# The MLP of a hybrid decoder layer on one core: order of the early products, engine of the weight sums, steps of splits and loads

## The chip, the cores and the metric

One core of a Trainium2 chip. The metric is device microseconds of one execution of the whole layer, the median of several runs. The engines are TensorE (PE: matmuls, and its weight loads PEld), VectorE (DVE, `V` in the code), ScalarE (ACT, `S`), GpSimd (POOL, `G`) and SyncE (SP, `SY`), which issues all the DMAs of this kernel. Each engine takes its instructions in the order in which the program gives them, so an instruction that waits holds up all that stand behind it on its engine.

## The reference

One decoder layer on 1024 tokens of width 1024, in float32: an attention mixture and an RWKV-7 branch, merged by gates, then a squared-ReLU MLP of width 4096, then a gated embedding per layer. The change touches the MLP alone:

```python
h = h + rmsnorm(merged @ w_out[i], mix_post_norm[i])
f = rmsnorm(h, ffn_pre_norm[i])
f = jnp.square(jax.nn.relu(f @ w_ff_in[i])) @ w_ff_out[i]   # 1024x1024 @ 1024x4096, 1024x4096 @ 4096x1024
h = h + rmsnorm(f, ffn_post_norm[i])
e = (p[i] @ w_ple[i]) * jax.nn.sigmoid(h @ w_ple_gate[i])
h = h + rmsnorm(e, ple_post_norm[i])
```

## The kernel before

**Precision.** Each float32 operand is split into a high part, rounded by ScalarE (`S.activation(hi, raw, Copy)` into fp32r), and a low part, `raw - hi`, by VectorE or GpSimd. A product is three matmuls (`mm3`, L289: high by high, high by low, low by high; lines 292, 294, 296), each 128x128 by 128x512.

**Seven products.** Both layers of the MLP are cut in two by two blocks and multiplied with seven products in place of eight, over sums of blocks. The hidden width is cut into 16 rows p of 256 (`NP`). In the first layer the products of a row are 1 and 2, and then 6, 5, 7, 3, 4 (`SEQ`), of four times three matmuls each. Products 1 and 2 need only tokens 0 to 511 and unchanged weights, so they are made early for all rows (`early`, L1555), while tokens 512 to 1023 are still on their way through `mixed` and `put_f`. 27 of the 32 come before anything else of the MLP, and the last five between the products of row 0. The outcome of product 1 goes to memory (`p1_scr`), product 2 is added to it in the same PSUM bank, and the result, after relu and square, goes to `c_scr`. So a bank is held from (p,1) to (p,2). Before, the order is (p,1), (p+1,1), (p,2), (p+1,2), and three banks take turns (`bank`, L1244).

`put_f` (L1418) makes, for each tile of 128 tokens from 512 on, the operands F[3] to F[7] out of the transposed tile: sums on VectorE (d, t2) and GpSimd (c, t4, two steps each), and a split of each by ScalarE and one of the two.

**The main loop** (`mlp`, L1652) goes over p = 1 to 15. TensorE makes row p's five other products in 20 chunks of three matmuls (`chunks`, L1631; `first`, L1598), and between them the second layer of row e = p - 1. For even e that is seven products over four token tiles (`seven`, L1828), for odd e four plain ones in eight steps u of two tiles (`plain`, L1847). Results go to five PSUM banks in turn (`XB`, L1825), from which VectorE adds them to totals in SBUF (tile `tot`). The first product of `FIRST` takes a new bank for each of the four token tiles.

`prep(n + 2)` (L1798), at the start of product n, prepares operands two products ahead into one of three pairs of tiles (`rooms`): the left one from `operand` (L1778; sums of blocks of hidden values on VectorE), split by ScalarE and GpSimd; the right one, for products 6, 5, 7 and 4, loaded from `bs_scr`, where `w2_sums` (L1755) had put the split sums of blocks of w_ff2's rows. `w2_sums` runs in six parts for the next even row during the plain products: parts 0 and 3 make two sums each on GpSimd, the others split one sum and store it. For p = 0 it runs in `beside` (L1576), among the early products.

**Deferred work.** What must not hold up an engine at once goes on the list `pend`; `flush` (L1481) runs the list after every chunk and every token tile. `part` (L1868) fills pauses with work for the end of the layer: it loads a piece of other weights (x = 0) and one step later splits and stores it (x = 1; ScalarE, VectorE, SP), through the two buffers of tile tag "gst". `take` (L1646) loads the next row's hidden values so far, `load_w2` (L1733) a row's two tiles of w_ff2, `w1_raw` and `w1_sum` the blocks of w_ff_in and their sums, `last_split` (L1717) the operands of the last row, whose second layer is `ff2_last` (L1888).

**Order.** A planner (`Order`, L136) emits all this with estimated times: dense work, and chains beside it that start when due (`yield` of a time). It sets TensorE's order throughout, and SP's from the early products on; with row 0's first product (L1663) all engines follow the written order.

Of the kernel before, what the change touches and what calls it, by code (L numbers as in the profile page):

```python
# [244 lines left out]
def layer(ctx: ExitStack, tc: tile.TileContext, x, pT, wz, wup, w_out, wff1, w_ff2, w_ple, w_pleg,  # L245
# [1151 lines left out]
    def mixed(i, ps):  # L1397
# [83 lines left out]
    def flush():  # L1481
        while pend:
            pend.pop(0)()
# [26 lines left out]
    for p in range(0, NP, 2):  # L1510
        early_ += [(p, 1), (p + 1, 1), (p, 2), (p + 1, 2)]
# [14 lines left out]
    def w1_split(j):  # L1526
# [7 lines left out]
        lo = lambda: (V if j < NA and j % 4 == 3 else G).tensor_tensor(w[:, 1], src, w[:, 0], OP.subtract)  # L1534
# [20 lines left out]
    def early(j):  # L1555
# [8 lines left out]
        if i == 1:  # L1564
            A_[p] = bank()
# [8 lines left out]
        SY.dma_start((p1_scr if i == 1 else c_scr)[p], dst)  # L1574

    def beside(j):  # L1576
# [10 lines left out]
        if j == 19:  # L1587
            load_w2(0)
# [4 lines left out]
        if j in (24, 26, 27, 28, 30, 32):  # L1593
            w2_sums(0, (24, 26, 27, 28, 30, 32).index(j))
# [57 lines left out]
    def mlp():  # L1652
# [11 lines left out]
        last["turn"].__enter__()  # L1664
        for n in range(5):
# [8 lines left out]
        flush()  # L1674
        for p in range(1, NP):
            Y["n"] = 0
            e = p - 1
            if e % 2 == 0:
                for x in range(7):
                    yield from chunks((20 * x + 23) // 7 if p < NP - 1 else (3, 6, 9, 13, 17, 20, 20)[x])  # L1680
                    yield from seven(items.index((e, x)))
                    if x == 0:
                        load_w2(p)
                    if x == 4:
                        take(p + 1)
                    if p == NP - 1:
# [6 lines left out]
            for u in range(8):  # L1693
                yield from chunks((20 * u + 23) // 8)
# [9 lines left out]
        flush()  # L1704
# [12 lines left out]
    def last_split(k, hs, ws):  # L1717

        if k not in last:
            if k == 0:  # L1720
                last["h"] = rtile([128, 4, 512], "lh", "BK", F32R)
                last["w"] = [rtile([128, 1024], "lw", t, F32R) for t in ("r", "k")]
            last[k] = (rtile([128, 2, 512], "lhl", ("Ep", "En")[k], F32R),
                       rtile([128, 1024], "lwl", ("kk", "MP")[k], F32R))
        for h in hs:
            x = 2 * k + h
            S.activation(last["h"][:, x], raw_h[NP - 1][:, x], AF.Copy)
            V.tensor_tensor(last[k][0][:, h], raw_h[NP - 1][:, x], last["h"][:, x], OP.subtract)
        for _ in ws:
            SY.dma_start(last["w"][k].bitcast(F32), pk[2][:, k, 0])  # L1730
            SY.dma_start(last[k][1].bitcast(F32), pk[2][:, k, 1])

    def load_w2(p):  # L1733
        if p == NP - 1:
            return
        raw_w[p] = [rtile([128, 1024], "w2r", ("r", "k", "MP")[(2 * p + k) % 3]) for k in range(2)]
# [18 lines left out]
    def w2_sums(p, n):  # L1755
# [6 lines left out]
        if n == 0:  # L1762
            G.tensor_tensor(t1, b[1], b[0], OP.subtract)
            G.tensor_tensor(t2, b[3], t1, OP.subtract)
            return
        if n == 3:
            G.tensor_tensor(t1, b[3], b[1], OP.subtract)
            G.tensor_tensor(t2, b[2], t2, OP.subtract)
            return
        x = n - 1 - (n > 3)  # L1770
        d = split2((t2, t1, t1, t2)[x], rooms(p)[1][x % 2], G)
        if p == 0:
            flush()
# [397 lines left out]
```

## Time and profile before

| | |
|---|---|
| timed runs | 1838.38, 1847.18, 1848.96 us; median 1847.18 |
| profiled execution | 1837.83 us, span 1836.0 us |
| PE | 1753.1 us busy (95%) |
| DVE, ACT, POOL | 1051.2 (57%), 751.6 (41%), 776.8 (42%) us busy |
| granted clock of TensorE, mean | 0.983 |
| DMA queue of SP | 240.98 MB, 38.0% of 16 engines' time |

A view of the profile lists the instructions by line of the code and tile names, `out<-in`; all of ACT, DVE and POOL's have line L113, the planner's helper, so they are told apart by their tiles: `wa`, `wr`, `w2r` are raw weights of the first and second layer, `wh`, `wl` split first-layer weights, `f`, `c`, `d`, `t` the tiles of `put_f`, `pa` the copies of early products, `duo` a split operand of the second layer, `sum` a sum of blocks, `bs` the store of split sums, `hr` hidden values, `gp`, `gph` the pieces of `part`. A wait is written "waiter <- who ended it". A stretch without stalls shows what TensorE needs for a matmul, and a window's length less its count times that is what it lost.

### The profile page before, as it was taken

To read this page: it belongs to the slowest core of one execution; us is meant where nothing else is said; L and a number is where in the kernel's file an instruction comes from. 1 tells how busy PE (TensorE), PEld (TensorE's weight loads), DVE (VectorE), ACT (ScalarE), POOL (GpSimd) and SP (SyncE) were. 2 spreads that over 40 slices of the span, in tenths; PEclk is the share of its full clock that TensorE was granted. 3 is DMA by queue.
4 is the path that set the end of the run, shared out by engine and by line. 5 is a ranking of instruction groups with operands and counts; after the bars stand their busy time and mean duration, and the time that the engine had idled before them with its cause. 6 is when DMAs were issued, how large, how long until landed. Compare 5 with 4: busy or idle time off the path is not lost.

```text
span 1836.0 us, 26373 instructions
## 1 busy us (share of the span) xinstructions
PE 1753.1 (95%) x10084; PEld 1417.0 (77%) x10084; DVE 1051.2 (57%) x1799; ACT 751.6 (41%) x1377; POOL 776.8 (42%) x532
## 2 busy tenths in 40 slices
PE   9999999999999999999998799998999989898998
PEld 8887777878877777778787687877877768676887
DVE  6289768586443333436538404575666756657743
ACT  5824423513244434534424544333343333333453
POOL 1343221221222323332303767767677676773211
PEclk9999999999999999999999999999999999999999
DMA  4521122113332222335413474546455464456611
GB/s 157 204 92 36 50 78 89 45 59 109 112 110 72 58 58 81 113 131 175 146 49 101 162 264 165 188 140 241 165 178 178 154 234 157 163 181 258 240 40 53
DMA packets 99392, 242.66 MB, mean 132 GB/s; under 512 B 11329, under 2 KB 11713, under 8 KB 98754
## 3 DMA queue, kind: packets, MB, share of 16 engines
q1 hardware_dynamic: 99266, 240.98, 38.0%
q8 instruction: 79, 1.29, 0.3%
q14 instruction: 47, 0.39, 0.1%
HBM read 167.14 MB, written 67.11 MB: 128 GB/s over the span
## 4 chain that ended last, share of the span: by engine, by line
PE 63%; DVE 10%; DMA 8%; POOL 8%; ACT 5%; issue 4%; SPq 1%; POOLq 0%; DVEq 0%; ACTq 0%
PE z L294 13%; PE z L296 13%; PE z L292 13%; PE bk L292 4%; PE bk L294 4%; PE bk L296 4%; DMA duo<-bs 2%; DVE tot L113 2%; DMA hr<-cscr 2%; POOL duo L113 2%; SPq L132 1%; POOL wh L113 1%; POOL wl L113 1%; PE sc L275 1%; DVE g L113 1%
## 5 line engine op out<-in xcount | busy, mean ns | idle before, releaser
L292 PE MATMUL z<-uh,wh 128*128 128x512 f32 (+1 forms) x800 | 313.0, 391 | 6.2 <-ACT part L113 3.0
L294 PE MATMUL z<-ul,wh 128*128 128x512 f32 (+1 forms) x800 | 314.7, 393 | 1.3 <-DVE ul L113 1.3
L296 PE MATMUL z<-uh,wl 128*128 128x512 f32 (+1 forms) x800 | 313.2, 392 | 2.7 <-POOL wl L113 2.7
L113 POOL TENSOR_TENSOR wl<-wr,wh 128x1024 fp32r<-128x1024 f32 (+1 forms) x56 | 133.0, 2375 | 420.9 <-ACT wh L113 401.7
L113 DVE TENSOR_TENSOR tot<-tot,bk 128x512 f32<-128x512 f32 x336 | 217.5, 680 | 52.6 <-PE bk L296 52.4
L292 PEld LDWEIGHTS z<-uh,wh 128*128 128x128 f32 x800 | 151.6, 189 | 37.4 <-ACT part L113 3.5
L296 PEld LDWEIGHTS z<-uh,wl 128*128 128x128 f32 x800 | 151.6, 190 | 34.3 <-POOL wl L113 4.0
L294 PEld LDWEIGHTS z<-ul,wh 128*128 128x128 f32 x800 | 151.7, 190 | 32.1 <-issue 3.6
L292 PE MATMUL bk<-duo 128*128 128x512 f32 x224 | 94.9, 424 | 33.1 <-DMA duo<-bs 16.9
L113 ACT ACTIVATE wh<-wr 128x1024 fp32r<-128x1024 f32 (+2 forms) x94 | 81.0, 861 | 100.9 <-PE z L294 55.9
L113 ACT ACTIVATE hr<-hr 128x512 f32<-128x512 f32 x96 | 60.7, 632 | 134.0 <-DVE hr L113 132.5
L113 POOL TENSOR_TENSOR duo<-sum,duo 128x512 fp32r<-128x512 f32 x64 | 89.0, 1395 | 25.6 <-ACT duo L113 24.9
L113 DVE TENSOR_TENSOR gp<-gp,gph 128x512 fp32r<-128x512 f32 x28 | 32.9, 1175 | 115.8 <-ACT gph L113 92.3
L113 ACT ACTIVATE duo<-sum 128x512 fp32r<-128x512 f32 x64 | 39.9, 623 | 135.3 <-POOL sum L113 77.0
L294 PE MATMUL bk<-duo 128*128 128x512 f32 x224 | 91.8, 410 | 1.6 <-POOL duo L113 1.6
L296 PE MATMUL bk<-duo 128*128 128x512 f32 x224 | 91.6, 409 | 0.0
L292 PE MATMUL bk<-ws,duo 128*128 128x512 f32 x224 | 87.1, 389 | 0.0
L294 PE MATMUL bk<-ws,duo 128*128 128x512 f32 x224 | 87.1, 389 | 0.0
L296 PE MATMUL bk<-ws,duo 128*128 128x512 f32 x224 | 87.1, 389 | 0.0
L292 PEld LDWEIGHTS bk<-duo 128*128 128x128 f32 x224 | 44.2, 197 | 55.6 <-DVE tot L113 25.0
L113 DVE TENSOR_TENSOR hr<-hr,z 128x512 f32<-128x512 f32 x80 | 54.3, 679 | 51.0 <-PE z L296 29.2
L292 PE MATMUL z<-f,wh 128*128 128x512 f32 x212 | 83.1, 392 | 0.0
(364 smaller groups left out, 4212.8 us busy)
## 6 DMA issues: line engine op xcount, KB each, us to landing
wr<-in_wz_dram SPq DMA_DIRECT2D x48, 512.0 KB, 3.7
bs<-duo SPq DMA_DIRECT2D x32, 512.0 KB, 3.0
duo<-bs SPq DMA_DIRECT2D x32, 512.0 KB, 4.1
w2r<-in_w_ff_dram SPq DMA_DIRECT2D x30, 512.0 KB, 6.4
wr<-in_wff_dram SPq DMA_DIRECT2D x56, 256.0 KB, 4.4
hr<-p1scr SPq DMA_DIRECT2D x48, 256.0 KB, 6.7
xt<-in_x_dram SPq DMA_DIRECT2D x16, 512.0 KB, 3.8
gscr<-gst SPq DMA_DIRECT2D x32, 256.0 KB, 2.1
```

The lines of the kernel that those rows point to most:

```text
L113: return f(*a, **kw)
L132: self.eng.dma_start(out_, in_)
L275: PE.matmul(out_, a, b, start=start, stop=stop)
L292: PE.matmul(ps, ah, bh, start=start and i == 0, stop=False, skip_group_check=not start)
L294: PE.matmul(ps, ah, bl, start=False, stop=False, skip_group_check=not start)
L296: PE.matmul(ps, al, bh, start=False, stop=i == n - 1, skip_group_check=not start)
```

## The change

The diff, cut:

```diff
@@ mixed, put_f
+        yield from wait(lambda: i < 5 or i - 1 in t_f)
         yield from put_f(hh, i)
...
         for n, x, eng in ((7, d, V), (6, t2, V), (5, c, G), (4, t4, G)):
+            if n in (6, 5):
+                yield 2.0
             S.activation(at(n, 0), x, AF.Copy)
@@ flush
-        while pend:
-            pend.pop(0)()
+        run = pend[:]
+        pend.clear()
+        for job in run:
+            job()
@@ early products
-    for p in range(0, NP, 2):
-        early_ += [(p, 1), (p + 1, 1), (p, 2), (p + 1, 2)]
+    for p in range(0, NP, 4):
+        early_ += [(p + q, i) for i in (1, 2) for q in range(4)]
...
-        lo = lambda: (V if j < NA and j % 4 == 3 else G).tensor_tensor(w[:, 1], src, w[:, 0], OP.subtract)
+        eng = V if k is not None and (j > 20 or j % 4 == 3) else G
+        lo = lambda: eng.tensor_tensor(w[:, 1], src, w[:, 0], OP.subtract)
...
-            A_[p] = bank()
+            if p == 0:
+                za, zb, zc = (("z0", "z1", "s0")[(zn[0] + n) % 3] for n in (1, 2, 3))
+                A_["tags"] = ("s1", "s2", "s3", za, zb, "s1", "s2", "s3", zc, za, zb, "s1", "s2", "s3", "s1", zc)
+            A_[p] = psum.tile([128, 512], F32, name="bk", tag=A_["tags"][p])
@@ sums ahead
+    AHEAD = (4, 2, 0)
+    steps = [(0, -1), (0, 0), (1, -1)] + [(0, n) for n in range(1, 6)] + [(1, 0), (2, -1)] + [
+        (1, n) for n in range(1, 6)] + [(2, n) for n in range(6)]
+    def ahead_(n):
+        for _ in range(n):
+            if steps:
+                q, x = steps.pop(0)
+                if x < 0:
+                    load_w2(AHEAD[q], ("kk", "v") if q == 1 else ("r", "k"))
+                else:
+                    w2_sums(AHEAD[q], x, ("a", "px", "Ep", "En"))
+                    for _ in range(3):
+                        flush()
@@ beside
-        if j == 19:
-            load_w2(0)
...
-        if j in (24, 26, 27, 28, 30, 32):
-            w2_sums(0, (24, 26, 27, 28, 30, 32).index(j))
+        if sch.t > t_f.get(7, 1e9) + 2.0:
+            ahead_(2 if j % 3 == 0 else 1)
+        if j == NA + 9:
+            ahead_(99)
@@ mlp, even e (seven products)
-                    if x == 0:
+                    if x == 2:
                         load_w2(p)
...
                     if p == NP - 1:
+                        if x in (0, 1):
+                            last_w(x, 0, "rk"[x])
                         if x in (1, 2, 5):
                             e_weights((1, 2, 5).index(x))
+                        if x == 4:
+                            last_w(0, 1, "En")
+                            last_w(1, 1, "MP")
+                            last_split(0, (0, 1))
                         if x == 5:
-                            last_split(0, (0, 1), (0,))
-                            last_split(1, (1, 0), (1,))
+                            last_split(1, (1, 0))
@@ mlp, odd e (four plain products)
             for u in range(8):
+                if u % 2 == 0:
+                    flush()
+                    part(2 * p - 4 + u // 2, 0)
                 yield from chunks((20 * u + 23) // 8)
-                if u == 0:
+                if u == (2 if p in AHEAD else 0):
                     load_w2(p)
                 yield from plain(items.index((e, u // 2)), u % 2)
-                if u == 1:
+                if u == 3:
                     take(p + 1)
-                    w2_sums(p, 0)
-                if 0 < u < 6:
-                    w2_sums(p, u)
-                part(2 * p - 4 + u // 2, u % 2)
+                if p in AHEAD:
+                    if u == 3:
+                        fetch(p, 6)
+                else:
+                    if u == 1:
+                        w2_sums(p, 0)
+                    if 0 < u < 6:
+                        w2_sums(p, u)
+                if u % 2:
+                    part(2 * p - 4 + u // 2, 1)
@@ w2_sums (all four sums and the low halves: G becomes V; the store is put off by two flushes)
-            G.tensor_tensor(t1, b[1], b[0], OP.subtract)
-            G.tensor_tensor(t2, b[3], t1, OP.subtract)
+            V.tensor_tensor(t1, b[1], b[0], OP.subtract)
+            V.tensor_tensor(t2, b[3], t1, OP.subtract)
...
-        d = split2((t2, t1, t1, t2)[x], rooms(p)[1][x % 2], G)
+        d = split2((t2, t1, t1, t2)[x], tags[x] if tags else rooms(p)[1][x % 2], V)
+        store = lambda: SY.dma_start(bs_scr[p, (6, 5, 7, 4)[x]], d.bitcast(F32))
+        pend.append(lambda: pend.append(store))
@@ operand (products 6, 3, 7: sums, high part, low part, each one flush later)
+        def sums():
...
+            t = ops["a", i]
+            def high():
+                S.activation(d[:, 0], t, AF.Copy)
+                pend.append(lambda: G.tensor_tensor(d[:, 1], t, d[:, 0], OP.subtract))
+            pend.append(high)
+        pend.append(sums)
@@ part
         S.activation(hi, raw, AF.Copy)
-        V.tensor_tensor(lo, raw, hi, OP.subtract)
-        SY.dma_start(dst[:, k, 0, c], hi.bitcast(F32))
-        SY.dma_start(dst[:, k, 1, c], lo.bitcast(F32))
+        def low():
+            V.tensor_tensor(lo, raw, hi, OP.subtract)
+            SY.dma_start(dst[:, k, 0, c], hi.bitcast(F32))
+            SY.dma_start(dst[:, k, 1, c], lo.bitcast(F32))
+        pend.append(low)
```

In words. (a) Early products go by four rows, product 1 of all four and then product 2, in six banks; `put_f` waits for the tile before it and pauses twice; ten more low halves of early weights go to VectorE. (b) `w2_sums` runs on VectorE. For rows 4, 2 and 0 it runs ahead, among the last early products and row 0's; rows 2 and 4 load their weights again for the plain use. (c) `flush` runs only what was on the list when it began, so that work put off twice runs a chunk or a tile later: the sums, the high and the low part of `operand`, the low part and the stores of `part`, the stores of `w2_sums`. (d) Loads move: `take` and `load_w2` by two steps, `part`'s load to the start of its step, product 6's operand of rows 2 and 4 to step 3 (`fetch`), the last row's operands from product step 5 to 0, 1 and 4.

More of the change, by code (lines that the diff above doesn't have):

```diff
@@ L1673, in mlp @@
         prep(1)
-        flush()
+        for _ in range(4):
+            flush()
         for p in range(1, NP):
@@ L1715, in mlp_ahead, with last_w, last_split @@
             a_raw(5)
[L1717 to L1724, printed above, removed]
+    def last_w(k, lo, tag):
+        t = rtile([128, 1024], "lw", tag, F32R)
+        last["w", k, lo] = t
+        SY.dma_start(t.bitcast(F32), pk[2][:, k, lo])
+    def last_split(k, hs):
+        if k == 0:
+            last["h"] = rtile([128, 4, 512], "lh", "BK", F32R)
+        last[k] = rtile([128, 2, 512], "lhl", ("Ep", "kk")[k], F32R)
         for h in hs:
@@ L1727, in last_split, with load_w2 @@
             S.activation(last["h"][:, x], raw_h[NP - 1][:, x], AF.Copy)
[L1728 to L1733, printed above, removed]
+            V.tensor_tensor(last[k][:, h], raw_h[NP - 1][:, x], last["h"][:, x], OP.subtract)
+    def load_w2(p, tags=None):
         if p == NP - 1:
             return
-        raw_w[p] = [rtile([128, 1024], "w2r", ("r", "k", "MP")[(2 * p + k) % 3]) for k in range(2)]
+        tags = tags or [("r", "k", "MP")[(2 * p + k) % 3] for k in range(2)]
+        raw_w[p] = [rtile([128, 1024], "w2r", t) for t in tags]
         for k in (0, 1):
@@ L1769, in w2_sums @@
             return
         x = n - 1 - (n > 3)
-        d = split2((t2, t1, t1, t2)[x], rooms(p)[1][x % 2], G)
-        if p == 0:
-            flush()
-            SY.dma_start(bs_scr[p, (6, 5, 7, 4)[x]], d.bitcast(F32))
-        else:
-            pend.append(lambda: SY.dma_start(bs_scr[p, (6, 5, 7, 4)[x]], d.bitcast(F32)))
-    def operand(p, i):
+        d = split2((t2, t1, t1, t2)[x], tags[x] if tags else rooms(p)[1][x % 2], V)
+        store = lambda: SY.dma_start(bs_scr[p, (6, 5, 7, 4)[x]], d.bitcast(F32))
@@ L1780, in operand, with fetch @@
+        pend.append(lambda: pend.append(store))
+    def fetch(e, i):
+        b = rtile([128, 2, 512], "duo", rooms(e)[MUL.index(i) % 3][1], F32R)
+        SY.dma_start(b.bitcast(F32), bs_scr[e, i])
+        ops["b", e, i] = b
+    def operand(p, i, tag):
         a = [raw_h[p][:, x] for x in (0, 2, 1, 3)]
         if i in (1, 2, 4):
-            return a[{1: 0, 2: 1, 4: 3}[i]]
-        if i == 6:
-            s1, s2 = (rtile([128, 512], "sum", x) for x in ("ex", "py"))
-            V.tensor_tensor(s1, a[2], a[3], OP.add)
-            V.tensor_tensor(s2, s1, a[0], OP.subtract)
-            ops["a", 5], ops["a", 6] = s1, s2
@@ L1788, in operand @@
-        if i == 3:
-            ops["a", 3] = rtile([128, 512], "sum", "ex")
-            V.tensor_tensor(ops["a", 3], a[1], ops["a", 6], OP.subtract)
-        if i == 7:
-            ops["a", 7] = rtile([128, 512], "sum", "py")
-            V.tensor_tensor(ops["a", 7], a[0], a[2], OP.subtract)
-        return ops["a", i]
+            return split2(a[{1: 0, 2: 1, 4: 3}[i]], tag, G)
+        if i == 5:
+            return split2(ops["a", 5], tag, G)
+        d = rtile([128, 2, 512], "duo", tag, F32R)
@@ new lines, in sums @@
+        def sums():
+            if i == 6:
+                s1, s2 = (rtile([128, 512], "sum", x) for x in ("ex", "py"))
+                V.tensor_tensor(s1, a[2], a[3], OP.add)
+                V.tensor_tensor(s2, s1, a[0], OP.subtract)
+                ops["a", 5], ops["a", 6] = s1, s2
+            if i == 3:
+                ops["a", 3] = rtile([128, 512], "sum", "ex")
+                V.tensor_tensor(ops["a", 3], a[1], ops["a", 6], OP.subtract)
+            if i == 7:
+                ops["a", 7] = rtile([128, 512], "sum", "py")
+                V.tensor_tensor(ops["a", 7], a[0], a[2], OP.subtract)
+            t = ops["a", i]
[3 more added lines that the diff above has]
+            pend.append(high)
@@ L1796, in layer @@
+        pend.append(sums)
+        return d
     items = [(e, x) for e in range(NP - 1) for x in range(4 if e % 2 else 7)]
@@ L1803, in prep @@
             i, room = MUL[x], rooms(e)[x % 3]
-            a = split2(operand(e, i), room[0], G)
+            a = operand(e, i, room[0])
             if i in (2, 1, 3):
@@ L1807, in prep @@
             else:
-                b = rtile([128, 2, 512], "duo", room[1], F32R)
-                SY.dma_start(b.bitcast(F32), bs_scr[e, i])
+                if ("b", e, i) not in ops:
+                    fetch(e, i)
+                b = ops["b", e, i]
             duo[n] = a, b
@@ L1891, in body @@
             ps = bank()
-            yield from mm3(ps, [(last["h"][:, 2 * k + h, ts], last[k][0][:, h, ts], last["w"][k][:, halves[c]],
-                                 last[k][1][:, halves[c]]) for k in range(2)])
+            yield from mm3(ps, [(last["h"][:, 2 * k + h, ts], last[k][:, h, ts], last["w", k, 0][:, halves[c]],
+                                 last["w", k, 1][:, halves[c]]) for k in range(2)])
             V.tensor_tensor(acc(i, c), acc(i, c), ps, OP.add)
```

11 lines of the change are left out of this document (7 added, 4 removed).

## Prediction

> **What bounds the kernel now.** I read the page first, then the table of windows over the MLP (989 to 1691 us), then TensorE's waits in each window, then the engines' timelines around two of its stalls.
>
> ```profile
> span 1836.0 us, 26373 instructions
> ```
>
> The profiled execution took 1837.8 us, 1.8 us more than its span; the median of the three timed runs, 1847.2, lies 9.4 above it and the lowest, 1838.4, 0.5 above. The columns of the next rows are length, then busy time (count) of PE, its weight loads, DVE, ACT and POOL, the granted clock, DMA share and GB/s.
>
> ```profile
> 989.00:1060.00 71.00, 55.40 (x221) 42.97 (x221) 40.26 (x41) 36.48 (x74) 54.18 (x36) 0.90 0.38 126
> 1060.00:1121.50 61.50, 58.91 (x259) 47.95 (x257) 6.28 (x9) 31.56 (x57) 43.16 (x34) 1.00 0.66 231
> 1121.50:1193.40 71.90, 69.22 (x301) 56.27 (x301) 45.75 (x60) 26.08 (x46) 55.48 (x42) 1.00 0.51 182
> 1193.40:1651.00 457.60, 428.42 (x1804) 344.69 (x1802) 295.57 (x396) 164.18 (x288) 324.39 (x240) 0.97 0.51 179
> 1651.00:1691.00 40.00, 33.57 (x140) 26.07 (x140) 31.34 (x47) 13.86 (x25) 16.00 (x12) 0.99 0.62 232
> 1216.25:1268.30 52.05, 52.01 (x229) 42.72 (x228) 30.80 (x40) 19.81 (x36) 36.50 (x27) 1.00 0.44 157
> ```
> ```profile
> L283 PE MATMUL tp<-cs,hh 128*128 128x128 f32 x24 | 3.6, 272 | 0.0
> ```
>
> The last row of the table is a stretch without stalls: 229 matmuls in 52.05 us, 0.2273 us each. At that pitch each window has a time it needs, and the rest is what the change can win. 989 to 1060: 221 less 24 transposes (3.6 us) is 197 x 0.2273 + 3.6 = 48.4, so 22.6 lost of 71.0. 1060 to 1121.5: 259 x 0.2273 = 58.9, 2.6 lost. 1121.5 to 1193.4: 68.4, 3.5 lost. 1193.4 to 1651: 410.0, 47.6 lost. 1651 to 1691: 31.8, 8.2 lost. Together 84.5 us. TensorE sets the time, and only its stalls can be shortened, since the change removes no matmul. Who ended them, by window (total, times, longest):
>
> ```profile
> PE bk L292 <- ACT pa L113: 15.6, 7, 5.5
> ```
> ```profile
> PE z L296 <- POOL wl L113: 1.8, 1, 1.8
> PE bk L294 <- POOL duo L113: 1.6, 1, 1.6
> ```
> ```profile
> PE bk L292 <- DMA duo<-bs: 16.1, 6, 3.6
> PE bk L292 <- DVE tot L113: 12.1, 6, 2.5
> ```
> ```profile
> PE bk L292 <- DVE tot L113: 3.8, 2, 2.6
> PE bk L294 <- DMA lwl<-pkl: 1.4, 2, 0.7
> PE bk L292 <- DMA lw<-pkl: 1.1, 1, 1.1
> ```
>
> These are 989 to 1060, 1060 to 1193.4, 1193.4 to 1650 and 1650 to 1691. So there are four places: the early products wait for ACT's copies out of PSUM; and each pair of rows in the main loop (six in the fourth window, about 76 us each) has one wait for DVE and one for a load, 2.0 and 2.7 us; then the end.
>
> Part of the loss is a low clock after a stall:
>
> ```profile
> 1207.73 0.47 PE L292 MATMUL bk<-duo 128*128 128x512 f32 x1 [2.50 <-DMA duo<-bs]
> ...
> 1210.08 0.63 PE L294 MATMUL bk<-duo 128*128 128x512 f32 x1
> 1210.50 0.63 PE L296 MATMUL bk<-duo 128*128 128x512 f32 x1
> ```
>
> The starts are 0.42 us apart after a gap of 2.50. In the main loop the waits make 28.2 of the 47.6; I count the other 19.4 mostly as this and as going with the stalls. The Trainium skill (TensorE: Matmul & The Clock Gate, "HAM oscillation") asks only that no idle gap be longer than about 3.4 us. By that rule gaps of 2.5 us would leave the clock alone and removing them would win the 28.2 and not the 19.4; the rows show slow matmuls right behind such a gap, so I go by the rows.
>
> **The change part by part.**
>
> Early products (22.6 lost). ACT is what is waited for, and its own waits in this window say why:
>
> ```profile
> ACT f L113 <- POOL t L113: 12.4, 4, 3.5
> ACT f L113 <- POOL c L113: 9.9, 4, 3.0
> ```
>
> ACT stands for GpSimd's four-step chain of each token tile (put_f), with the copies "pa" queued behind it. Now (p,2) follows (p,1) after one other product, 12 x 0.2273 = 2.7 us; in fours it follows after three, 8.2 us, and a bank comes round after four or more. ACT standing 3.5 us then costs nothing. The pauses of 2.0 us in put_f put other ACT work between the pieces, and the wait for the tile before spreads the chains; the last tile gets perhaps 10 us later in the plan, still under the 27 products (27 x 2.7 = 74 us) that cover it. What is late next is GpSimd: 54.18 of 71.0 busy, 36 instructions at 1.5 us. The same work in 48 us doesn't fit, though some of it may fall behind 1060, and the low halves of the weights are in its queue. Bounds: 0 (GpSimd keeps the pace as it is) to 22.6 won; I take 14, nearer the upper end, since what PE waited for here was never GpSimd directly.
>
> Sums of weights, 1060 to 1121.5. Three sets (p = 4, 2, 0) instead of one are made here, by DVE, which is busy 6.28 of 61.5 us. Each set is four sums and four low halves:
>
> ```profile
> L113 POOL TENSOR_TENSOR sum<-w2r 128x512 f32<-128x512 f32 x12 | 15.5, 1289 | 33.1 <-DMA w2r<-in_w_ff_dram 33.1
> L113 POOL TENSOR_TENSOR duo<-sum,duo 128x512 fp32r<-128x512 f32 x48 | 67.4, 1409 | 20.2 <-ACT duo L113 20.2
> ```
> ```profile
> L113 DVE TENSOR_TENSOR tot<-tot,bk 128x512 f32<-128x512 f32 x264 | 170.8, 680 | 41.8 <-PE bk L296 41.6
> L113 DVE TENSOR_TENSOR sum<-sum,hr 128x512 f32<-128x512 f32 x6 | 9.9, 1643 | 0.2
> ```
>
> Eight on DVE cost 5.4 us (0.68) to 13.1 us (1.643), so 24 cost 16 to 39 us, and hide behind 55 idle ones. The Trainium skill speaks against the move (SBUF — State Buffer, "Who interferes with whom"): a VectorE instruction with two inputs in SBUF and a GpSimd instruction that reads it exclude each other, and the later one stands for the whole of the other. The rows agree in sign, 0.680 with one input in PSUM against 1.643 with both in SBUF; by the rule one sum costs up to 0.68 + 1.29 = 1.97, eight 15.8, still hidden.
>
> The bill here is the transfers: two more sets are 2 MB of loads again (the main loop still loads them) and 4 MB of stores, 6 MB on top of 231 GB/s x 61.5 us = 14.2 MB. The share 0.66 becomes 0.66 x 20.2 / 14.2 = 0.94. The early weights, one 256 KB load per product, are needed within some 8 us. DVE stands in order for the first set's load; behind it are low halves of early weights (DVE gets ten more of them, 0.7 to 1.6 us each, from GpSimd), three or more products ahead of their use, and TensorE waits for those. SP stands for each set's low halves with the early loads behind it. Bounds: 2.6 won (SP's load for p = 0 leaves the crowded place) to 8 lost (the 6 MB take 17 us at the full rate, 231 / 0.66 = 350 GB/s, and half shows). I take 2.5 lost.
>
> At 1121.5 the first real operands wait for ACT and GpSimd; GpSimd is freed of eight operations, which takes the 1.8 and part of the 1.6. Won: 0 to 3.5, I take 1.5.
>
> Main loop (47.6 lost). One stall, read backwards in the four engines' timelines:
>
> ```profile
> 1244.93 1.29 POOL L113 TENSOR_TENSOR sum<-w2r 128x512 f32<-128x512 f32 x1 [5.94 <-DMA w2r<-in_w_ff_dram]
> ```
> ```profile
> 1263.33 0.63 ACT L113 ACTIVATE wh<-wr 128x512 fp32r<-128x512 f32 x1 [2.86 <-POOL wr L113]
> 1263.87 0.61 ACT L113 ACTIVATE duo<-sum 128x512 fp32r<-128x512 f32 x1
> ```
> ```profile
> 1265.04 1.32 DVE L113 TENSOR_TENSOR gp<-gp,gph 128x512 fp32r<-128x512 f32 x1 [5.07 <-ACT gph L113]
> ...
> 1268.31 1.00 DVE L113 TENSOR_TENSOR sum<-hr 128x512 f32<-128x512 f32 x1 [1.36 <-ACT hr L113]
> ...
> 1270.91 1.27 DVE L113 TENSOR_TENSOR tot<-tot,bk 128x512 f32<-128x512 f32 x2
> ```
>
> GpSimd stands 5.94 us for the rows of w_ff2 and is late for the rest of the four plain products; ACT waits for its sum, DVE in "part" for ACT, then in "operand" for ACT again, and the adds that free the banks come at 1270.91, while the next row's first product wants four new banks. The change cuts each link: the eight operations leave GpSimd (4 x 1.29 + 4 x 1.41 = 10.8 us per pair of rows), the low half in "part" and the sums in "operand" step back by one flush or two, so that DVE passes the adds first, and the load of "part" starts a step earlier. DVE gets 5.4 to 13.1 us more on 49 of 76. It will now stand for the rows itself:
>
> ```profile
> 1248.80 1.37 DVE L113 TENSOR_TENSOR gp<-gp,gph 128x512 fp32r<-128x512 f32 x1 [8.16 <-DMA hr<-p1scr]
> ```
>
> It stood 8.16 us at the same place already, without a stall on TensorE, so 5.9 us and the two sums behind it are covered by the five banks. If that cover were gone, each us beyond it costs one per pair of rows, five times (p = 6 to 14).
>
> The second stall is SP's order:
>
> ```profile
> 1270.46 0.32 SPq L132 DMA_DIRECT2D duo<-bs  x1
> ...
> 1276.93 2.22 SPq L132 DMA_DIRECT2D wr<-in_wff_dram  x3
> 1279.19 0.43 SPq L132 DMA_DIRECT2D duo<-bs  x1
> ```
> ```profile
> duo<-bs SPq DMA_DIRECT2D x32, 512.0 KB, 4.1
> w2r<-in_w_ff_dram SPq DMA_DIRECT2D x30, 512.0 KB, 6.4
> ```
>
> The operand issued at 1279.19 is used in the third product, planned at 1277.9 (two products and their chunks, 42 matmuls, behind 1268.3); it lands 4.1 later. Before it stand the stores of "part" and three weight loads that wait for GpSimd. With GpSimd in time and the stores a step apart, its room is free at 1268.3, and it must be issued by 1273.8; I reckon with some 5 us behind the preparation. A wait is new: "part" now loads right behind the stores that free its buffer, so SP stands about 2 us for a store, with fetches behind it that have 10. The other moves have one answer, nothing: the loads of the next row's hidden values (four of 256 KB) and of an odd row's w_ff2 (two of 512 KB) go out two steps, 9 us, later and are used three or more products later; the first operand load of p = 2 and 4 goes out earlier; if a moved load should be late, its landing, 6.4 us, is the price once per row. Bounds for the loop: a loss of 45 (the DVE rival below) to all 47.6 won. Six pairs keeping 1 to 2 us each leaves 10 or so; I take 36 won.
>
> The end (8.2 lost). The 2 MB of the last operands are issued two products earlier; that takes the 2.5 of loads, and the new order of sums most of the 3.8. Won: 0 to 8.2, I take 5.
>
> Sum: -14 + 2.5 - 1.5 - 36 - 5 = -54. From the profiled time that is 1784; from the median 1793. I forecast 1788, between the two.
>
> **The rivals.** (1) The load stays late: at the third product SP still waits for GpSimd's low half before the wr loads. For it: the three wr loads stay ahead of it; against: the cause of GpSimd's lateness is removed. The 16.1 and the same share of the low clock (16.1 / 28.2 x 19.4 = 11) stay: 1788 + 27 = 1815. (2) GpSimd is the bound of the early products at once: nothing is won there, 1788 + 14 = 1802. (3) Slower: DVE, in order, becomes what GpSimd was. Place: the wait for w_ff2's rows in the plain products. If SP's new waits move that load back by about one step (5 us) and sums cost 1.64, DVE stands 5.9 + 5 + 3.3 = 14 us where 8.2 + 1.4 was still covered; the 4.6 beyond that and as much low clock, 9 x 5 pairs = 45, come on top of stalls that then stay as they are. From a stand of 9.6 us it decides. 1788 + 36 + 45 = 1869. Against it: 49 of 76 busy. (4) The change doesn't do what it says: the stalls are moved by a step and return, 1838 to 1847.
>
> **How the numbers follow.** Forecast 0.61, (1) 0.15, (2) 0.10, (3) 0.06, (4) 0.08. The forecast's own range is 1765 to 1808, from 23 more won (the early stage and the loop nearly whole) to 20 less. To hold eight in ten it has to take in (2) and most of (1): 1764 to 1826. A measurement of this kernel tells about 1%, 18 us, from no change: faster by more 0.85, within 0.08, slower 0.07.
>
> **What would show it.** Right: in 1193 to 1651 the waits for "tot" and "duo<-bs" go from 28 us to under 8, GpSimd's wait for w2r is gone and DVE has one of some 6 us at the same place, which stalls nothing; the early window loses under 10 and waits for "wh" or "wl" of GpSimd, not "pa". Between 1060 and 1121 the DMA share is near 0.9 and a wait for "wa" may stand. Wrong: "duo<-bs" as large as before, or DVE's waits for w2r followed by PE's waits for "tot".

## The result, and the profile after

The changed kernel took 1799.6 us (median of four runs, 1797.0 to 1802.0). The kernel before, run beside it, took 1847.9 (four runs, 1838.4 to 1849.0). The ratio is 0.9749, with a 95% interval from 0.9714 to 0.9784: faster, 11.6 us behind the forecast of 1788 and inside its range. The profiled execution took 1800.1 us.

```profile
span 1798.3 us, 26359 instructions
```

The span fell by 37.7 us, the median by 48.3: the execution that was profiled before lay at the low end of its runs, the one after in the middle. What follows compares the profiled executions. The table of windows, with edges at the changed kernel's own stages (columns as in the prediction: length, PE, weight loads, DVE, ACT, POOL, granted clock, DMA share, GB/s), and the row of the transposes:

```profile
989.00:1060.00 71.00, 62.42 (x266) 49.45 (x265) 43.62 (x42) 41.03 (x81) 55.16 (x37) 0.95 0.43 147
1060.00:1121.50 61.50, 55.31 (x224) 42.94 (x224) 34.22 (x43) 33.72 (x60) 26.67 (x20) 0.94 0.87 322
1121.50:1325.00 203.50, 203.36 (x895) 167.37 (x894) 147.68 (x199) 74.72 (x130) 127.26 (x94) 1.00 0.51 175
1325.00:1620.00 295.00, 281.65 (x1201) 227.23 (x1200) 214.95 (x297) 109.73 (x192) 173.30 (x129) 0.98 0.53 185
1620.00:1656.00 36.00, 34.12 (x147) 27.02 (x146) 31.09 (x47) 14.78 (x27) 15.26 (x12) 1.00 0.71 258
```
```profile
L283 PE MATMUL tp<-cs,hh 128*128 128x128 f32 x24 | 3.8, 282 | 0.0
```

At the pitch of 0.2273 us the five windows lost 12.2 (266 less 24 is 242 x 0.2273 + 3.8 = 58.8 of 71.0), 10.6, 0.1, 22.0 and 2.6 us: 47.5, where the kernel before lost 84.5. The third window is the surprise: 203.5 us, the start of the main loop and its rows 2 and 4, without a stall. The rest is in three places, and the waits of TensorE there are these (total, times, longest; first 989 to 1060, then 1060 to 1121.5, then 1325 to 1620):

```profile
PE bk L292 <- ACT pa L113: 3.7, 1, 3.7
PE bk L296 <- POOL wl L113: 2.6, 1, 2.6
PE bk L296 <- POOL wh L113: 2.3, 3, 1.1
```
```profile
PE bk L292 <- ACT wh L113: 3.8, 1, 3.8
```
```profile
PE bk L292 <- DMA duo<-bs: 8.9, 4, 2.6
PE bk L292 <- DVE tot L113: 4.3, 9, 1.1
```

The 15.6 us for "pa" became 3.7, and GpSimd's low halves stand behind it. The crowded stretch has a wait that it did not have, for the high part of an early weight. The loop's two waits have the same names as before, now in four rows of six: 13.2 us where there were 28.2.

To compare kernels by stage, every profile was cut at four events: the first early product, the first product of the second layer ("early" ends), the first product on the last row's operands ("loop" ends), and the end. The pairs are the six pairs of rows from (2, 3) to (12, 13). Times in us; ratios are to the runs of the kernel before beside the same group.

| kernel | early | loop | tail | pairs of rows | median | ratio, 95% interval |
|---|---|---|---|---|---|---|
| before | 133.0 | 563.7 | 150.2 | 74.9 75.8 75.3 75.2 77.9 77.9 | 1847.9 | |
| the change | 129.1 | 533.9 | 146.4 | 68.4 68.4 74.4 74.8 72.1 73.8 | 1799.6 | 0.9749, 0.9714 to 0.9784 |
| e_nosums | 128.5 | 509.4 | 146.8 | 68.3 to 68.4 | 1777.4 | 0.9652, 0.9628 to 0.9677 |
| e_w2early | 128.4 | 515.2 | 147.2 | 68.3 68.4 68.7 72.3 69.0 69.3 | 1780.4 | 0.9671, 0.9649 to 0.9693 |
| e_bs5first | 128.5 | 518.4 | 146.9 | 68.4 68.4 69.8 72.5 70.5 68.8 | 1783.6 | 0.9688, 0.9665 to 0.9710 |
| e_both | 126.6 | 510.0 | 146.8 | 68.3 | 1776.6 | 0.9631, 0.9597 to 0.9666 |
| e_gsums | 128.6 | 538.2 | 146.9 | 68.3 68.5 73.1 75.9 74.2 74.8 | 1807.5 | 0.9796, 0.9760 to 0.9831 |
| e_flush | 128.1 | 535.7 | 146.8 | 68.3 68.3 76.1 74.2 72.7 74.6 | 1800.3 | 0.9769, 0.9727 to 0.9811 |
| e_pairs | 132.4 | 534.2 | 146.5 | 68.4 68.4 72.4 74.5 72.4 74.7 | 1804.8 | 0.9821, 0.9774 to 0.9867 |
| e_row0 | 131.5 | 545.5 | 146.8 | 72.7 73.1 74.6 73.4 73.6 75.0 | 1814.4 | 0.9841, 0.9796 to 0.9885 |
| e_row0b | 120.1 | 546.9 | 146.9 | 72.9 75.1 74.7 75.0 72.2 74.6 | 1805.0 | 0.9786, 0.9753 to 0.9819 |
| e_early_v | 123.1 | 534.7 | 146.5 | 68.4 68.3 72.9 74.7 74.9 74.7 | 1791.0 | 0.9713, 0.9679 to 0.9747 |
| e_step | 125.9 | 538.1 | 146.9 | 68.4 68.4 74.7 74.7 74.3 75.6 | 1801.3 | 0.9765, 0.9731 to 0.9799 |
| e_best | 122.9 | 509.8 | 146.2 | 68.3 to 68.4 | 1770.5 | 0.9601, 0.9572 to 0.9631 |

How far such lengths repeat can be read in the table. The kernels whose early products are the change's own have 126.6 to 129.1 there; the four with its loop (the change, e_pairs, e_early_v, e_step) have 533.9 to 538.1, and 294.0 to 299.4 for the last four pairs together; loops without a stall have 509.4 to 510.0. What lies ahead of the MLP, which no edit touches, ended between 984.6 and 992.5, and that is in every total.

### The profile page after: what moved, and what is told of

Same layout as the page of the kernel before. It is cut to its first block, busy times and chain, and to the rows that moved or that the text cites. A ratio compares the mean times of both kernels' runs of the same rounds, so it can differ in the third digit from the quotient of the medians.

```text
span 1798.3 us, 26359 instructions
## 1 busy us (share of the span) xinstructions
PE 1741.8 (97%) x10084; PEld 1410.6 (78%) x10084; DVE 1100.8 (61%) x1873; ACT 753.1 (42%) x1377; POOL 682.1 (38%) x458
## 4 chain that ended last, share of the span: by engine, by line
PE 66%; DVE 9%; DMA 9%; ACT 5%; POOL 4%; issue 4%; SPq 2%; DVEq 0%; ACTq 0%; POOLq 0%
PE z L294 13%; PE z L296 13%; PE z L292 13%; PE bk L292 5%; PE bk L294 5%; PE bk L296 5%; SPq L132 2%; DMA w2r<-in_w_ff_dram 1%; DVE tot L113 1%; DMA duo<-bs 1%; PE sc L275 1%; DMA wa<-in_wff_dram 1%; DVE xy L113 1%; PE A L275 1%; PE y L275 1%
## 5 line engine op out<-in xcount | busy, mean ns | idle before, releaser
L292 PE MATMUL bk<-duo 128*128 128x512 f32 x224 | 91.4, 408 | 14.9 <-DMA duo<-bs 8.9
L294 PE MATMUL bk<-duo 128*128 128x512 f32 x224 | 89.6, 400 | 0.2 <-POOL duo L113 0.2
L296 PE MATMUL bk<-duo 128*128 128x512 f32 x224 | 89.4, 399 | 0.0
L292 PE MATMUL z<-f,wh 128*128 128x512 f32 x212 | 83.1, 392 | 2.2 <-ACT pa L113 2.2
L296 PE MATMUL z<-f,wh 128*128 128x512 f32 x212 | 83.0, 392 | 0.0
L294 PE MATMUL z<-f,wh 128*128 128x512 f32 x212 | 82.9, 391 | 0.0
L113 POOL TENSOR_TENSOR wh<-wr,wh 128x512 fp32r<-128x512 f32 x38 | 53.9, 1421 | 67.3 <-ACT wh L113 55.8
```

Of the source, the lines that this page charges most:

```text
L113: return f(*a, **kw)
L292: PE.matmul(ps, ah, bh, start=start and i == 0, stop=False, skip_group_check=not start)
L294: PE.matmul(ps, ah, bl, start=False, stop=False, skip_group_check=not start)
L296: PE.matmul(ps, al, bh, start=False, stop=i == n - 1, skip_group_check=not start)
```

## The experiments

### What is left in the main loop

The theory was a chain that starts with the sums made in the loop. VectorE stands for w_ff2's rows, then for ScalarE's high part of each sum, and is late for all that is behind; ScalarE stands for VectorE in turn; `part` and SP are late with them, and the load of product 5's right operand, behind `part`'s stores on SP, lands late. VectorE's waits and ScalarE's, 1325 to 1620, in the changed kernel:

```profile
DVE duo L113 <- ACT duo L113: 24.2, 18, 2.4
DVE sum L113 <- DMA w2r<-in_w_ff_dram: 18.1, 8, 4.4
```
```profile
ACT duo L113 <- DVE sum L113: 79.8, 16, 10.1
```

SyncE's issues in one row, whose product 1 began at 1324.2, and what came of the third operand load in it:

```profile
1326.06 0.32 SPq L132 DMA_DIRECT2D duo<-bs  x1
1328.89 0.32 SPq L132 DMA_DIRECT2D pkl<-gph  x1
1329.62 0.32 SPq L132 DMA_DIRECT2D pkl<-gp  x1
1330.79 1.29 SPq L132 DMA_DIRECT2D wr<-in_wff_dram  x3
1332.18 0.38 SPq L132 DMA_DIRECT2D duo<-bs  x1
```
```profile
1338.01 0.65 PE L292 MATMUL bk<-duo 128*128 128x512 f32 x1 [2.56 <-DMA duo<-bs]
```

The load went out 8.0 us behind the row's start and landed 5.7 us after that, and TensorE had stood for 2.56.

**e_nosums.** Rows 6 to 14 make no sums and take the operands that row 4 stored, so their outputs are of other numbers; the loads of w_ff2 stay.

```diff
-                else:
-                    if u == 1:
-                        w2_sums(p, 0)
-                    if 0 < u < 6:
-                        w2_sums(p, u)
...
-        SY.dma_start(b.bitcast(F32), bs_scr[e, i])
+        SY.dma_start(b.bitcast(F32), bs_scr[min(e, 4), i])
```

> Leaves out the sums of weights of rows 6 to 14 altogether (their four operands are taken from row 4's store, so the output is not the reference's). Theory A (in these rows DVE and ACT stand for w_ff2's rows and pass the lateness on to the stores and loads ahead of the operand load): the waits for duo<-bs and for tot vanish in all rows as they did in rows 2 and 4; about 20 us less, 1780. Rival B (SP's order alone, the weight loads and part's stores ahead of the operand load): the waits for duo<-bs stay at about 2 us in each of four rows, and under 6 us are won.

TensorE's longest wait from 1180 to 1640:

```profile
PE bk L294 <- DMA lw<-pkl: 0.6, 1, 0.6
```

The loop took 509.4, 24.5 less, and both waits are gone together, as theory A has it. The window there had lost 22.0, so all that was left hangs on the sums with their splits and stores.

**e_bs5first.** Product 5's operand is loaded one product earlier, ahead of `part`'s stores on SP.

```diff
                 for x in range(7):
+                    if x == 0 and e:
+                        fetch(e, 5)
```

> The operand load of the third product (product 5) is issued ahead of the first product's chunks, so before part's stores and the three weight loads on SP. Theory A (lateness of the chain, SP's order is only its last link): the load goes out some 5 us earlier, duo<-bs waits vanish, tot waits of about 1 us per row stay: 4 times 2.4 us and as much again of low clock, 14 us less in all, 1786. Rival B (the load is held by its room or by the traffic): under 4 us won.

TensorE's waits from 1180 to 1640, and the new place of the load on SP:

```profile
PE bk L292 <- DVE tot L113: 5.0, 9, 1.8
PE bk L292 <- DMA duo<-bs: 0.6, 1, 0.6
```
```profile
1324.02 0.80 SPq L132 DMA_DIRECT2D duo<-bs  x2
```

Over that stretch the change itself has 8.9 for the load and 5.7 for "tot". The load now goes out about 2 us behind its row's start (1322.3 in this run), and its wait is nearly gone; that for VectorE stays, and VectorE stands for w_ff2's rows as long as before (21.2 us in ten waits against 22.6). The loop fell by 15.5 us: the last link of the chain alone was cut. That is more than the wait that went, 8.3; low clock behind the stalls is part of it (see the end).

**e_w2early.** The first link: w_ff2's rows of p = 6 to 14 are loaded one step earlier, at the end of the seven products.

```diff
+                    if x == 6 and p > 4 and p < NP - 1:
+                        load_w2(p + 1)
...
-                if u == (2 if p in AHEAD else 0):
+                if u == 2 and p in AHEAD:
                     load_w2(p)
```

> For rows 6 to 14 the two loads of w_ff2's rows are issued at the end of the last of the seven products before, about 3 us earlier in the order and ahead of the weight loads on which SP waits. Theory A (DVE's stand for w_ff2's rows, 18 us in four rows, starts the lateness): the stand vanishes, the tot waits too, and duo<-bs waits fall to under half; 10 to 20 us less, 1780 to 1790. Rival B (the stand is covered and the stall comes from SP's order): DVE's stand vanishes and the time stays within 4 us of 1800.

VectorE no longer waits for the rows at all. SP's issues and TensorE's waits (1180 to 1640):

```profile
1324.33 0.32 SPq L132 DMA_DIRECT2D pkl<-gp  x1
1325.50 1.28 SPq L132 DMA_DIRECT2D wr<-in_wff_dram  x3
1326.88 0.38 SPq L132 DMA_DIRECT2D duo<-bs  x1
```
```profile
PE bk L292 <- DMA duo<-bs: 2.8, 2, 2.1
```

Product 1 of this row began at 1322.2, so the operand's load went out 4.7 us behind it, where it was 8.0. Nothing about the stores or that load was edited, and both moved up by the same 3.3 us. So the chain runs from the late rows, over VectorE and `part`, to SP. The loop fell by 18.7 us.

**e_both.** Both edits.

```diff
+                    if x == 0 and e:
+                        fetch(e, 5)
...
+                    if x == 6 and p > 4 and p < NP - 1:
+                        load_w2(p + 1)
...
-                if u == (2 if p in AHEAD else 0):
+                if u == 2 and p in AHEAD:
```

> Both: product 5's operand load ahead of the first product's chunks, and the loads of w_ff2's rows at the end of the seven products. Theory A (two causes in a row, DVE's stand and SP's order): all stalls in rows 6 to 14 go but parts of a us, 3 to 6 us below the better of the two alone (0.9671), ratio 0.964 to 0.966. Rival B (one cause, each removal takes all of it that can be had): the same as the better one within 2 us.

TensorE's longest wait from 1125 to 1650:

```profile
PE bk L294 <- DMA lw<-pkl: 0.5, 1, 0.5
```

The loop took 510.0, as without sums, and 23.9 less than the change. The gains of the two edits do not add up (15.5 + 18.7), as two links of one chain don't. But neither edit alone takes all of it: together they win 5.2 us more than the earlier rows alone, within the 3 to 6 of theory A, so SP's order still costs something when the rows are early. With both edits the sums cost nothing that the loop shows (509.4 without them).

**e_gsums.** In the loop the sums go back to GpSimd; ahead they stay on VectorE.

```diff
+        E = V if tags else G
-            V.tensor_tensor(t1, b[1], b[0], OP.subtract)
+            E.tensor_tensor(t1, b[1], b[0], OP.subtract)
...
-        d = split2((t2, t1, t1, t2)[x], tags[x] if tags else rooms(p)[1][x % 2], V)
+        d = split2((t2, t1, t1, t2)[x], tags[x] if tags else rooms(p)[1][x % 2], E)
```

> In the loop, rows 6 to 14, the sums of weights and their low halves are on GpSimd again; the sets made ahead stay on DVE. Theory A (the wait for w_ff2's rows starts the lateness, whichever engine stands for it; GpSimd's sums take twice as long): stalls of tot come back to about 2 us per row and duo<-bs stays, 2 to 3 us more per row, 10 us slower than the change in all, ratio about 0.980. Rival B (the engine doesn't matter, the deferral does the work): within 3 us of the change.

TensorE's waits, 1125 to 1650:

```profile
PE bk L292 <- DMA duo<-bs: 9.3, 5, 2.5
PE bk L292 <- DVE tot L113: 7.8, 10, 1.9
```

The ratio is the one that theory A gave, but its interval overlaps the change's. By the profiles the loop was 4.3 longer, less than half of what was expected, and e_step, whose loop is the change's own, had 538.1 too; 2.6 more lie ahead of the MLP. So by the loop which engine makes the sums decides little here, 0 to 4 us: whichever does stands for the rows (GpSimd 26.3 us in four waits from 1325 to 1620) and is late.

**e_flush.** `flush` empties the whole list again, so the steps of part (c) run in one go.

```diff
-        run = pend[:]
-        pend.clear()
-        for job in run:
-            job()
+        while pend:
+            pend.pop(0)()
```

> The list of deferred work is run to its end at each flush again, so that sums, high and low parts and stores follow each other at once. Theory A (the steps are what lets DVE pass the adds that free the banks): tot waits of 1 to 2.5 us at the first of the seven products return in rows 6 to 14 and small ones in rows 2 and 4; 6 to 12 us slower than the change, ratio 0.979 to 0.982. Rival B (the steps cost nothing and win nothing once GpSimd is not late): within 3 us of the change, ratio 0.974 to 0.976.

TensorE's wait for VectorE's adds, 1125 to 1650:

```profile
PE bk L292 <- DVE tot L113: 8.0, 10, 2.2
```

"tot" stalls a little more (5.7 in the change, 3.4 to 5.6 in the other three with its loop), the loop is 1.8 longer, inside the spread, and rows 2 and 4 run at 68.3 without the steps. The theory that the steps are what made them stall-free falls.

### The early products and the sums ahead

**e_pairs.** The early products by two rows and in three banks again, all else as changed.

```diff
-    for p in range(0, NP, 4):
-        early_ += [(p + q, i) for i in (1, 2) for q in range(4)]
+    for p in range(0, NP, 2):
+        early_ += [(p + q, i) for i in (1, 2) for q in range(2)]
...
-            A_[p] = psum.tile([128, 512], F32, name="bk", tag=A_["tags"][p])
+            A_[p] = bank()
```

> The changed kernel with the early products again by two rows in three banks; all else as changed. Theory A (banks were what ACT's copies stalled): the early stage, 989 us to the first operand of the main loop, gets longer by about 10 us, since TensorE's waits for the copies pa come back to some 12 us or more; 1800 becomes about 1810, and the rows of the main loop do not differ. Rival B (GpSimd's pace bounds the early products, the banks only move the wait): the stage gets longer by under 4 us and pa's waits replace waits for GpSimd's low halves.

TensorE's waits, 985 to 1125:

```profile
PE bk L292 <- ACT pa L113: 13.6, 4, 4.5
```

The wait for the copies is back, 9.9 us more, and the waits for GpSimd's low halves (4.9) are gone. The stage took 3.3 us longer. The wait is the one that theory A gave, the price that of rival B (under 4, one wait in place of the other): the order removes the wait that it was made for, and about half of that comes back as a wait for the next engine.

**e_row0 and e_row0b.** Sums ahead for row 0 only. In e_row0 the deferred list was left to the last products, and VectorE made two early weights' low halves late, behind the first matmuls that read them, so the output is of other numbers; a stall of 7.6 us for such a low half hides the rest. e_row0b empties the list once the steps are done.

```diff
-    AHEAD = (4, 2, 0)
-    steps = [(0, -1), (0, 0), (1, -1)] + [(0, n) for n in range(1, 6)] + [(1, 0), (2, -1)] + [
-        (1, n) for n in range(1, 6)] + [(2, n) for n in range(6)]
+    AHEAD = (0,)
+    steps = [(0, n) for n in range(-1, 6)]
...
+        if not steps:
+            for _ in range(3):
+                flush()
```

> Only row 0's sums of weights are made ahead; rows 2 and 4 make theirs in the loop as rows 6 to 14 do. Theory A (making sums ahead costs the early stage what it wins in the loop, or nearly): in 1060 to 1120 the stalls of 4.0 and 2.6 us on ACT's copies and splits and the low clock behind them go, about 8 us won there; rows 2 and 4 lose 5 to 6 us each as the later rows do, about 11; in sum 1 to 5 us slower than the change, ratio to before about 0.977. Rival B (those two stalls are not from the sums ahead): they stay, and the kernel is some 11 us slower, ratio 0.981.

> As the kernel with row 0's sums alone ahead, but with the list of deferred work run in each step of the early stage after them too, as the change does (there, two early weights had their low halves put after the first matmuls that read them). Theory A (each set made ahead wins its row 5 to 6 us in the loop and costs the early stage about 3): stalls between 1060 and 1120 under 4 us, rows 2 and 4 lose 5 to 6 us each; ratio 0.977 to 0.982. Rival B (the early stage does not profit): ratio above 0.983.

The last three lines of the diff are e_row0b's alone. Its row for the crowded window:

```profile
1060.00:1121.50 61.50, 59.44 (x261) 48.57 (x260) 28.48 (x37) 31.32 (x54) 34.15 (x26) 1.00 0.72 260
```

261 matmuls fit where 224 did, and DMA moves 260 GB/s, not 322. The early stage is 9.0 us shorter (120.1) and the loop 13.0 longer, with rows 2 and 4 at 72.9 and 75.1 like the others. So the sums ahead of rows 2 and 4 cost 9.0 and win 13.0 (11.2 in the two rows themselves, theory A's 5 to 6 each); the net of 4 is inside the two intervals, which overlap. It also prices the rest of the early edits: 133.0 to 120.1 is 12.9 us.

**e_early_v.** `put_f`'s four sums on VectorE.

```diff
-        G.tensor_tensor(c, c, at(1, 0), OP.subtract)
+        V.tensor_tensor(c, c, at(1, 0), OP.subtract)
...
-        G.tensor_tensor(t4, t4, at(2, 1), OP.add)
+        V.tensor_tensor(t4, t4, at(2, 1), OP.add)
```

> The changed kernel with the four sums on GpSimd in each token tile of put_f on DVE. Theory A (what is left of the early stalls is ACT and the low halves standing for GpSimd's chain): TensorE's waits for pa (3.7) and for GpSimd's low halves (4.9) between 985 and 1060 fall to under 3 in all; with the low clock 8 to 11 us less than the change, ratio 0.969 to 0.971. Rival B (DVE, with the norms of the next tokens in its queue, becomes the late one): the waits change their name, the time stays within 4 us, ratio 0.973 to 0.977.

TensorE's waits, 985 to 1125:

```profile
PE bk L296 <- DVE wl L113: 4.0, 1, 4.0
...
PE bk L296 <- POOL wh L113: 1.0, 1, 1.0
```

The stage fell by 6.0 us. The "pa" wait at its start is gone and GpSimd's 4.9 became 1.0, while VectorE's own low halves come late once: GpSimd was the bound there. The waits for ScalarE behind 1060 stay (3.0 for "wh", 2.3 for "pa"). The span fell by 9.2, but 4.2 of that lie ahead of the MLP, and the interval overlaps the change's.

**e_step.** In the sums ahead the list is run ahead of each step, once, and not three times behind it.

```diff
                 q, x = steps.pop(0)
+                flush()
...
-                    for _ in range(3):
-                        flush()
```

> The changed kernel with one run of the deferred list ahead of each step of the sums made ahead, in place of three behind it, so that a step's low half and store come one and two steps later. Theory A (the stalls at 1104 and 1112 come from DVE and ACT waiting for each other in each step): they fall from 6.0 us of waits to under 2, 5 to 8 us less with the low clock, ratio 0.970 to 0.972. Rival B (they come from DVE's stand for the last set's rows of w_ff2 and the full DMA queue): they stay, ratio 0.974 to 0.976.

The wait for "wh" went from 3.8 to 1.7, that for "pa" behind it stayed at 2.2, the stage went to 125.9, just below the spread, and the total did not move. Of the 6.0 us 3.9 are left, so theory A explains the smaller part. In e_row0b 0.7 is left, so the rest too comes with the sums ahead; by which way was not tried.

### The version from these

**e_best.** The diffs of e_both, e_early_v and e_step together, in short:

```diff
-        G.tensor_tensor(c, c, at(1, 0), OP.subtract)
+        V.tensor_tensor(c, c, at(1, 0), OP.subtract)
...
+                flush()
...
+                        fetch(e, 5)
```

> Both earlier loads in the loop, the sums of put_f on DVE, and the steps put off. If the theories A hold and add up, the MLP keeps under 10 us of stalls and the ratio is 0.952 to 0.957; if only the loop's two edits count, 0.963.

1770.5 us, 0.9601 (0.9572 to 0.9631): 4.0% faster than the kernel before, and its interval lies below that of the change. Against e_both it is not told apart (0.9597 to 0.9666). The loop is at 509.8. The early stage, 122.9, keeps these waits of TensorE above 1 us (985 to 1060, then 1060 to 1125):

```profile
PE bk L296 <- DVE wl L113: 3.8, 1, 3.8
```
```profile
PE z L292 <- ACT pa L113: 3.7, 1, 3.7
PE bk L292 <- ACT wh L113: 1.7, 1, 1.7
```

## Why the prediction was right, and where it was not

The sum was -54 from the profiled time; the profiles give -37.0. The median fell by 48.3, so the sum made from the median (1793) was 6 off and that from the profile (1784) 16; the forecast stood between them. By terms, lost before and after: early order 10.4 won (14 taken), sums ahead 8.0 lost (2.5 taken), loop with its start 29.0 won (37.5 taken), end 5.6 won (5 taken). The three large terms were all taken too favourably, so their errors add up. Of the signs that the prediction named, the loop's two waits came to 13.2 us and not to under 8, and the early window lost 12.2 and not under 10, with one wait for "pa" left; the DMA share near 0.9 held (0.87). VectorE's waits for w_ff2's rows, followed by TensorE's for "tot", were named as a sign of being wrong: they are there, and small (4.3 us for "tot").

**Early order: right, and a little large.** "What is late next is GpSimd" came true: its low halves stall TensorE for 4.9 us, and e_early_v shows it as the bound. The step that failed is "ACT standing 3.5 us then costs nothing". ScalarE in the changed kernel:

```profile
1005.88 0.63 ACT L113 ACTIVATE f<-c 128x512 fp32r<-128x512 f32 x1 [3.05 <-POOL c L113]
1008.10 0.63 ACT L113 ACTIVATE f<-t 128x512 fp32r<-128x512 f32 x1 [1.58 <-DVE t L113]
...
1012.67 0.63 ACT L113 ACTIVATE f<-t 128x512 fp32r<-128x512 f32 x1 [3.10 <-POOL t L113]
1013.21 0.58 ACT L113 ACTIVATE pa<-bk 128x512 f32<-128x512 f32 x1
```

It stood three times in a row, 7.7 us in 10, with the copy behind all three. Each stand alone was within the 8.2 us that the order in fours gives; their sum and the work between them were not. Without the extra sums ahead the early edits are worth 12.9 (e_row0b against before). The order by fours was worth 3.3 where it was undone alone (e_pairs, with the crowd); how the rest splits over the pauses, the ten low halves on VectorE and row 0's sums was not tried.

**Sums ahead: the sign right, the price wrong.** 2.5 was taken from bounds of -2.6 to 8; e_row0b gives 9.0, above the upper one. The expected DMA share was 0.94, measured 0.87. The step that failed is the one that let 24 operations "hide behind 55 idle ones": VectorE had the time, but not at the right moment. ScalarE and VectorE around the longest stall there:

```profile
1106.17 1.29 ACT L113 ACTIVATE hr<-hr 128x512 f32<-128x512 f32 x2 [5.41 <-DVE hr L113]
1107.36 0.61 ACT L113 ACTIVATE wh<-wa 128x512 fp32r<-128x512 f32 x1
```
```profile
1102.19 1.66 DVE L113 TENSOR_TENSOR sum<-w2r 128x512 f32<-128x512 f32 x1
1103.78 1.76 DVE L113 TENSOR_TENSOR sum<-w2r,sum 128x512 f32<-128x512 f32 x1
1105.46 0.67 DVE L113 TENSOR_TENSOR hr<-hr,z 128x512 f32<-128x512 f32 x1
```

Row 0's `hr` add stood behind a set of sums on VectorE; ScalarE waited 5.41 us for it, with the split of an early weight (`wh`) and the copies behind, and TensorE waited 3.8 for the split. What the sums gave back was put down in the prediction under the loop, where it is 13.0.

**Loop: the chain right, its cut incomplete.** The links named were the right ones (the rows of w_ff2, the split, `part`, the adds, SP's order), and e_w2early and e_bs5first cut them one at a time. The step that failed is "5.9 us and the two sums behind it are covered by the five banks". That held for the banks nearly: the "tot" stalls of that window are 1.1 us at most, 4.3 in all. It was not asked what else stands behind VectorE. VectorE in the changed kernel:

```profile
1300.40 0.69 DVE L113 TENSOR_TENSOR sum<-w2r 128x512 f32<-128x512 f32 x1 [3.88 <-DMA w2r<-in_w_ff_dram]
...
1318.39 1.37 DVE L113 TENSOR_TENSOR duo<-sum,duo 128x512 fp32r<-128x512 f32 x1 [2.43 <-ACT duo L113]
1319.68 1.78 DVE L113 TENSOR_TENSOR gp<-gp,gph 128x512 fp32r<-128x512 f32 x1
```

The piece of `part` (`gp`) is behind, and its stores stand before the operand's load, so "must be issued by 1273.8; I reckon with some 5 us" came out as 8.0, with a landing of 5.7 in place of 4.1. That is rival (1) in four rows of six, with the cause of rival (3) in small: VectorE, not GpSimd, was late. Its point of decision was set too high, at 9.6 us: stands of up to 4.4, each with a wait for ScalarE behind it, were enough, through SP and not through the banks. The other two rows escaped it because their sums were gone, not because of the cut links (with their sums back in e_row0b they take 72.9 and 75.1).

So nearly half of the loop's 29.8 (563.7 to 533.9) is rows 2 and 4, 13.9 us by their lengths. The other four pairs won 11.2, from 306.3 to 295.1, and 4.7 lie in the rows at both ends. In e_gsums the four pairs won 8.3, in e_flush 8.7: neither the engine nor the steps of the list, undone alone, takes back more than 3 us of it, and loops without such an edit differ by 5.4 there. The two were not undone together, nor the moved loads one by one, so what made this part is open.

**End: right.** The load waits are gone, and what is left of the window's waits is 1.4 us for "tot".

## What to carry to other kernels

When a stall is covered for the engine at the end of the chain, ask of every queue behind the waiting instruction what it issues next: here 4 us of waiting on VectorE cost little through PSUM (1.1 us at most) and made a load on SyncE late. Of a chain of waits, cut the first link (a load one step earlier) and the last (the load that is waited for ahead of the stores); changing the engine that passes it on decided little here (0 to 4 us). Work moved ahead into idle time is not free when each piece is longer than the slack of what stands behind it in order: price it by the longest set, not by the sum.

## What the runs showed of the hardware

**The clock after a gap of 2 us: slow in two cases of three.** From 1120 to 1685 us, in the profiles of before, the change, e_w2early, e_flush and e_gsums, ten stalls of TensorE lasted 1.0 to 1.7 us, and none was followed within 8 us by matmuls at half pace (starts 0.40 to 0.46 apart); of 22 from 1.8 to 2.7 us, 15 were, within 2.5 us; and all three of 3.4 to 3.6 us. What follows three gaps of the change, the first that of 2.56 at 1338.01:

```profile
1338.46 0.63 PE L294 MATMUL bk<-duo 128*128 128x512 f32 x1
...
1486.55 0.47 PE L292 MATMUL bk<-duo 128*128 128x512 f32 x1 [1.69 <-DMA duo<-bs]
1486.86 0.39 PE L294 MATMUL bk<-duo 128*128 128x512 f32 x1
...
1558.76 0.47 PE L292 MATMUL bk<-duo 128*128 128x512 f32 x1 [2.02 <-DMA duo<-bs]
...
1559.98 0.61 PE L296 MATMUL bk<-duo 128*128 128x512 f32 x1
1560.39 0.63 PE L292 MATMUL bk<-duo 128*128 128x512 f32 x1
```

After 2.56 the pace is 0.43 at once, after 1.69 not at all, after 2.02 it drops 1.2 us later. Each slow stretch has 5 to 8 matmuls and costs 1 to 1.6 us (0.20 each); the one behind the gap of 3.60 has 11. In the loop before there were 51 such matmuls, 10 us of the 19.4 that the prediction counted "mostly as this"; in the change 23, 4.6 us. The other 9 of the 19.4 were not followed up. The Trainium skill (TensorE: Matmul & The Clock Gate, "What's actually happening") describes a window of 3.4 us that runs freely and does not start with the kernel's work. A slow stretch of eight, 8 x 0.43 = 3.4 us, and its shifting start agree with that, the stretch of eleven does not; the limit of 3.4 us for one gap, which the prediction weighed, does not hold here, since a gap of 1.84 was enough.

**Two inputs in SBUF.** The sums on VectorE took 0.69 us with GpSimd idle (1300.40) and 1.66 and 1.76 at 1102.19 and 1103.78, while GpSimd had two of its own, from 1101.96 and here:

```profile
1103.38 1.61 POOL L113 TENSOR_TENSOR wr<-wr 128x512 f32<-128x512 f32 x1
```

In the loop they took 0.75 and 0.69 on the mean, the low end of what was allowed for.
